# Sliding-window attention scores in a two-block network: masks written first, two score heads per row half, four PSUM banks in turn

## The chip, the cores and the metric

The program runs on one core of a Trainium2 chip. The metric is the device time of one execution in microseconds (us). TensorE (PE in the profile) multiplies, VectorE (DVE), ScalarE (ACT) and GpSimd (POOL) do the elementwise work, SyncE (SP) issues most transfers. PSUM, where TensorE writes, has eight banks of 512 fp32 columns on 128 partitions.

## The reference

Two blocks work on 512 tokens of width 1024. The first block (a linear-recurrence mixer, sparse attention and a mixture of 64 experts) is not touched. The second block has two layers, each of a feed-forward network, a hybrid mixer and another feed-forward network. The mixer projects the normalised tokens to eight query heads of 64, two key and two value heads of 64, a recurrence and a short convolution; the outputs are concatenated and multiplied with `w_out`. Its attention is:

```
scores = einsum('bnqkgd,bnskd->bnkgqs', qb, kb) * 64 ** -0.5      # blocks of 128 queries, 256 keys
scores = where(in_window & valid, scores - slope[head] * dist, -1e30)
m = max(max(scores), sink);  p = exp(scores - m);  denom = sum(p) + exp(sink - m)
out = (p / denom) @ vb
y = concatenate([y_attn, y_lru, y_shortconv]) @ w_out
```

A query sees the 128 keys up to itself, so a block of 128 queries needs its own block of keys and the one before it; the first block needs its own alone.

## The kernel before

The activations lie transposed (features on partitions, 512 tokens on columns). Products with weights are made of three fp32r products (`mm3`, L160, L161, L162): weights and activations are each split into a high and a low part, by a cast on ACT (L166) and a subtraction on DVE (L167). `fm` accumulates one 128x512 projection over eight slices in a bank: 24 products.

`mixer` (L1629) runs once a layer. It projects the recurrence inputs, keys and values, the queries and then, in a loop over four query blocks, calls `swa` (L1757). After it come the six projections of the short convolution (144 products into `ps_fm`), its elementwise work on DVE (L1740 to L1747), and `down` (L1560), the product with `w_out` into `ps_dn` banks; that takes the slices in the order 0 to 3 (attention), 6, 7 (short convolution), 4, 5 (recurrence), the first 256 tokens before the last 256.

The layout of `swa`: query head t of key group 0 lies on partitions 0 to 63 of tile t of `q` (`mxa` in the profile), head t + 4, of group 1, on partitions 64 to 127. `kk` holds the keys of group 0 and 1 on the same halves. So a score product uses 64 of the array's 128 rows, either the lower or the upper half. `swab` holds the masks with the distance penalty, in bf16; a product with the bf16 identity (`identb`) adds a mask to scores in PSUM.

For two heads at a time, `swa` takes one `ps_dn` bank. For each head it makes the score product (L1767, fp32, which the profile shows as two passes) and then the mask product (L1768). DVE takes the maximum (`swm`, L1769) and the bias (`swn`, L1770), ACT the exponential with its sum (L1773). When all eight heads are through, the probabilities are scaled (group 0 on DVE, L1787; group 1 in four pieces on ACT, L1785), transposed on PE into `ps_sm` (L1792), copied to `pt` (L1794, on DVE or ACT), and multiplied with the values into `ps_po` (L1798), where each product uses 64 of the array's columns. The result is split into the operands of `w_out`.

PSUM holds three `fm` banks, two `dn`, two `sm` and one `po` in this part of the program. A bank is taken in turn: a new tile of a tag waits until the oldest one's readers are done.

The order of instructions on each engine isn't that of the source: a scheduler sets it when the program is built. Engines then run their queues in that order. In the program before, the scheduler puts the scores between the projections of the short convolution: these are written after `swa` in the source, but run while the softmax of a bank is under way.

Of the kernel before, what the change touches and what calls it, by code (L numbers as in the profile page):

```python
# [14 lines left out]
AF = mybir.ActivationFunctionType  # L15
OP = mybir.AluOpType
AX = mybir.AxisListType
# [124 lines left out]
class Kern:  # L142
# [1609 lines left out]
    def swa(self, l, i, q, kk, v, swab):  # L1752

        nc, d = self.nc, self.dpool
        t_ = slice(i * 128, (i + 1) * 128)
        j0 = max(i - 1, 0)
        nj = i + 1 - j0  # L1757
        nk = nj * 128
        mx, nm, sm = (d.tile([128, 8], F32, name=n, tag=n, bufs=2) for n in ("swm", "swn", "sws"))
        pp = [self.m4.tile([128, 4, 256], F32, name="swp", tag="macc", bufs=3) for _ in range(2)]  # L1760
        for h in range(0, 8, 2):
            ps = self.bank("dn")[:, 0:2 * nk].rearrange("p (t k) -> p t k", t=2)
            g = h // 4
            gp = slice(g * 64, (g + 1) * 64)
            for a in range(2):
                t = (h + a) % 4
                nc.tensor.matmul(ps[:, a], q[gp, t, t_], kk[gp, j0 * 128:(i + 1) * 128], start=True, stop=False)  # L1767
                nc.tensor.matmul(ps[:, a], self.identb, swab[:, t, g, 256 - nk:256], start=False, stop=True)  # L1768
            nc.vector.tensor_reduce(mx[:, h:h + 2], ps, AX.X, OP.max)  # L1769
            nc.vector.scalar_tensor_tensor(nm[:, h:h + 2], mx[:, h:h + 2], -0.125, self.nsink[:, l, h:h + 2],  # L1770
                                           op0=OP.mult, op1=OP.min)
            for a in range(2):
                nc.scalar.activation(pp[g][:, (h + a) % 4, 0:nk], ps[:, a], AF.Exp, bias=nm[:, h + a:h + a + 1],  # L1773
                                     scale=0.125, accum_out=sm[:, h + a:h + a + 1])
        nc.vector.tensor_tensor(mx, nm, self.sink[:, l], OP.add)
        nc.scalar.activation(mx, mx, AF.Exp)
        nc.vector.tensor_tensor(sm, sm, mx, OP.add)
        nc.vector.reciprocal(sm, sm)
        pso = self.bank("po")
        for g in range(2):  # L1780
            gp = slice(g * 64, (g + 1) * 64)
            pv = pp[g][:, :, 0:nk]
            if g:
                for t in range(4):
                    nc.scalar.mul(pv[:, t], pv[:, t], sm[:, 4 + t:5 + t])  # L1785
            else:
                nc.vector.tensor_tensor(pv, pv, sm[:, 0:4, None].to_broadcast([128, 4, nk]), OP.mult)  # L1787
            pts = []
            for j in range(nj):
                pst = self.bank("sm")  # L1790
                for n, t in enumerate((0, 2, 1, 3)):
                    nc.tensor.transpose(pst[:, n * 128:(n + 1) * 128], pp[g][:, t, j * 128:(j + 1) * 128], self.ident)  # L1792
                pt = self.t2("pt")
                (nc.scalar.copy if j else nc.vector.tensor_copy)(pt, pst)  # L1794
                pts.append(pt)
            for b in range(2):
                for j in range(nj):
                    nc.tensor.matmul(pso[b * 64:(b + 1) * 64, g * 256:(g + 1) * 256], v[:, j0 + j, gp],  # L1798
                                     pts[j][:, b * 256:(b + 1) * 256], start=j == 0, stop=j == nj - 1)
        self.split(pso[:].rearrange("p (k s) -> p k s", k=4), self.ah[:, 0:4, t_], self.al[:, 0:4, t_])  # L1800
# [112 lines left out]
```

## Time and profile before

| | us |
|---|---|
| three runs | 3186.16, 3207.44, 3209.56 (median 3207.44) |
| the profiled execution | 3204.98 |
| its span, first to last instruction | 3203.2 |
| PE busy in the span | 3079.4 (96%) |
| DVE busy | 1874.3 (59%) |
| ACT busy | 1263.3 (39%) |

The profile is of one execution; times within it count from the start of the span. Busy is the time in which at least one instruction of an engine ran. PE starts a product before the one ahead of it has ended, so the time that one takes from the others is read from start to start, not from its duration. The chain that ended last is PE for 85% of the span. Score products of the two layers start from 1735.0 to 1802.7 us and again from 2697 us.

### The profile page before, as it was taken

Reading aid. Unit: us, or ns where it says so; the run is one execution under the profiler, and the core shown is the slowest. Engines: PE = TensorE matmul, PEld = TensorE weight load, DVE = VectorE, ACT = ScalarE, POOL = GpSimd, SP = SyncE. Lnnn points to the kernel's source line nnn. Section 1 sums busy time; section 2 is a strip of 40 time slices with the busy share of each in tenths; the row PEclk is TensorE's granted clock in tenths of the full one; section 3 lists DMA queues with packets and bytes.
Section 4 is the critical chain, followed back from the end, with each engine's and each line's share of the span. In section 5 each row is a group of like instructions: output and inputs, shape, how many; then the busy total and the mean of one; then the engine's idle time right before and its main releaser. Section 6 shows DMA issues by size and latency. Waiting matters only on the chain.

```text
span 3203.2 us, 40592 instructions
## 1 busy us (share of the span) xinstructions
PE 3079.4 (96%) x15628; PEld 2352.7 (73%) x15629; DVE 1874.3 (59%) x3048; ACT 1263.3 (39%) x2048; POOL 338.8 (11%) x373
## 2 busy tenths in 40 slices
PE   6999998999999996999999999999999989999999
PEld 5987477555555653888887788889888887788888
DVE  6776558777777765544485654345444485653335
ACT  5135554444445544322245542224322244542323
POOL 0111001322232322000010000000000010000000
PEclk9998799999999998999999999999999999999999
DMA  6574146999899996454372335344344372232323
GB/s 240 180 230 149 47 138 246 320 345 339 292 334 346 335 328 217 148 158 133 125 243 81 123 123 157 125 145 132 119 151 139 125 230 79 87 109 95 105 81 104
DMA packets 317574, 576.57 MB, mean 180 GB/s; under 512 B 49488, under 2 KB 252048, under 8 KB 292800
## 3 DMA queue, kind: packets, MB, share of 16 engines
q1 hardware_dynamic: 268656, 434.99, 39.3%
q0 software_dynamic: 46640, 136.84, 14.7%
q8 instruction: 125, 2.05, 0.3%
q10 hardware_dynamic: 2080, 2.10, 0.2%
q14 instruction: 73, 0.60, 0.1%
HBM read 550.84 MB, written 28.39 MB: 181 GB/s over the span
## 4 chain that ended last, share of the span: by engine, by line
PE 85%; DVE 5%; DMA 5%; issue 3%; ACT 1%; POOL 0%; SPq 0%; DVEq 0%; ACTq 0%; POOLq 0%
PE ps_fm L161 12%; PE ps_fm L162 12%; PE ps_fm L160 12%; PE ps_dn L1327 6%; PE ps_dn L160 6%; PE ps_dn L162 6%; PE ps_dn L161 6%; PE ps_gu L160 3%; PE ps_gu L161 3%; PE ps_gu L162 3%; PE ps_sc L876 2%; PE ps_tr L1297 2%; PE ps_pj L161 2%; PE ps_pj L160 2%; PE ps_pj L162 2%
## 5 line engine op out<-in xcount | busy, mean ns | idle before, releaser
L167 DVE TENSOR_TENSOR wlo<-wraw,whi 128x1024 fp32r<-128x1024 f32 x480 | 566.4, 1183 | 656.3 <-ACT whi L166 649.7
L166 ACT CAST whi<-wraw 128x1024 fp32r<-128x1024 f32 x480 | 487.0, 1017 | 860.8 <-PE ps_fm L161 366.9
L160 PE MATMUL ps_fm<-dhh,whi 128*128 128x512 f32 (+1 forms) x1808 | 675.9, 377 | 8.7 <-ACT dhh L1513 6.4
L161 PE MATMUL ps_fm<-dhl,whi 128*128 128x512 f32 (+1 forms) x1808 | 676.5, 375 | 3.0 <-DVE dhl L1514 2.5
L162 PE MATMUL ps_fm<-dhh,wlo 128*128 128x512 f32 (+1 forms) x1808 | 663.1, 375 | 1.1 <-DVE wlo L167 1.0
L160 PEld LDWEIGHTS ps_fm<-dhh,whi 128*128 128x128 f32 x1808 | 342.2, 190 | 70.2 <-ACT dhh L1513 7.3
L161 PEld LDWEIGHTS ps_fm<-dhl,whi 128*128 128x128 f32 x1808 | 343.4, 190 | 64.3 <-DVE dhl L1514 4.6
L160 PE MATMUL ps_dn<-ah,whi 128*128 128x256 f32 (+1 forms) x1152 | 383.8, 334 | 5.4 <-DVE xT L1590 5.4
L162 PEld LDWEIGHTS ps_fm<-dhh,wlo 128*128 128x128 f32 x1808 | 343.5, 190 | 61.2 <-DVE wlo L167 1.9
L161 PE MATMUL ps_dn<-al,whi 128*128 128x256 f32 (+1 forms) x1152 | 382.4, 332 | 0.0
L162 PE MATMUL ps_dn<-ah,wlo 128*128 128x256 f32 (+1 forms) x1152 | 380.3, 334 | 0.0
L167 DVE TENSOR_TENSOR wlo<-wbig,whi 128x1024 fp32r<-128x1024 f32 x192 | 232.1, 1220 | 94.8 <-ACT whi L166 94.4
L160 PEld LDWEIGHTS ps_dn<-ah,whi 128*128 128x128 f32 x1152 | 216.4, 188 | 30.6 <-DVE xT L1590 3.7
L166 ACT CAST whi<-wbig 128x1024 fp32r<-128x1024 f32 x192 | 198.9, 1047 | 95.8 <-PE ps_gu L162 77.7
L161 PEld LDWEIGHTS ps_dn<-al,whi 128*128 128x128 f32 x1152 | 216.6, 188 | 26.1 <-issue 1.5
L162 PEld LDWEIGHTS ps_dn<-ah,wlo 128*128 128x128 f32 x1152 | 216.3, 188 | 23.5 <-issue 0.8
L161 PE MATMUL ps_gu<-wlo,th 128*128 128x512 f32 (+21 forms) x512 | 210.2, 411 | 10.9 <-DVE wlo L167 10.9
L160 PE MATMUL ps_gu<-whi,th 128*128 128x512 f32 (+21 forms) x512 | 210.5, 412 | 2.0 <-ACT whi L166 1.8
L162 PE MATMUL ps_gu<-whi,tl 128*128 128x512 f32 (+21 forms) x512 | 202.8, 396 | 0.0
L1590 DVE SCALAR_TENSOR_TENSOR xT<-ps_dn,modc,xT 128x256 f32<-128x256 f32 (+1 forms) x160 | 93.7, 589 | 161.7 <-PE ps_dn L162 161.5
L1327 PE MATMUL ps_dn<-dnraw,eaf 128*80 128x512 f32 (+20 forms) x368 | 167.4, 596 | 0.5 <-ACT eaf L976 0.5
L1198 POOL DMA_INDIRECT ring<-h2d,iidx x64 | 96.0, 1500 | 381.6 <-PE ps_tr L1297 130.3
(533 smaller groups left out, 4112.2 us busy)
## 6 DMA issues: line engine op xcount, KB each, us to landing
wbig<-in_w_exp_gu_dram SPq DMA_DIRECT2D x96, 1024.0 KB, 14.5
wraw<-in_w_ffn_gu_dram SPq DMA_DIRECT2D x86, 1024.0 KB, 5.1
dnraw<-in_w_exp_dn_dram SPq DMA_DIRECT2D x48, 1024.0 KB, 10.1
mw<-in_w_mod_dram POOLq DMA_DIRECT2D x80, 512.0 KB, 4.4
mraw<-in_w_mod_dram POOLq DMA_DIRECT2D x64, 512.0 KB, 4.7
wraw<-in_w_exp_gu_dram SPq DMA_DIRECT2D x32, 1024.0 KB, 12.6
wraw<-in_w_ffn_down_dram SPq DMA_DIRECT2D x32, 1024.0 KB, 5.0
wraw<-in_w_out_dram SPq DMA_DIRECT2D x24, 1024.0 KB, 5.0
```

The source lines that it names most:

```text
L160: mm(ps, ah, bh, start=first, stop=False)
L161: mm(ps, ah, bl, start=False, stop=False)
L162: return mm(ps, al, bh, start=False, stop=last)
L166: self.copied = self.nc.scalar.copy(hi, src)
L167: self.rest = self.nc.vector.tensor_tensor(lo, src, hi.bitcast(F32), OP.subtract)
L876: nc.tensor.matmul(ps[:, 0:nk], qr[gp, t, t_], self.kr[b][gp, 0:nk], start=True, stop=False)
L1198: self.nc.gpsimd.indirect_dma_start(out=g[0:cap], out_offset=None, in_=self.h2d[:], in_offset=bass.IndirectOffsetOnAxis(ap=i_ap[0:cap], ax ...
L1297: nc.tensor.transpose(ps[:, k * 128:k * 128 + m], g[0:m, 4 * a + k:D:8], self.ident[0:m, 0:m])
L1327: self.mark2 = nc.tensor.matmul(ps[0:m], af[:, k, 0:m], dv[:, k, cs], start=k == 0, stop=k == 1)
L1590: self.hold = nc.vector.scalar_tensor_tensor(self.xT[:, k, hs], ps[j], G[:, k:k + 1], self.xT[:, k, hs], op0=OP.mult, op1=OP.add)
```

## The change

`swa` goes over the heads in two rounds (c = 0 and 1) of four: heads 2c and 2c + 1 of group 0 and the same of group 1 (t and t + 4). It takes two banks a round, one for each group: `ps_dn` in the first round, `ps_fm` in the second. One mask product (L1765) now writes the masks of a bank's two heads at once and opens the accumulation, 512 columns wide (256 in the first query block). Then the score products (L1769) are written a head of group 0 and a head of group 1 in turn. Maxima, biases and exponentials are the same instructions, in another order.

```diff
-        for h in range(0, 8, 2):
-            ps = self.bank("dn")[:, 0:2 * nk].rearrange("p (t k) -> p t k", t=2)
-            g = h // 4
-            gp = slice(g * 64, (g + 1) * 64)
+        for c in range(2):
+
+            pss = [self.bank("fm" if c else "dn")[:, 0:2 * nk].rearrange("p (t k) -> p t k", t=2) for _ in range(2)]
+            for g in range(2):
+                nc.tensor.matmul(pss[g], self.identb, swab[:, 2 * c:2 * c + 2, g, 256 - nk:256], start=True, stop=False)
             for a in range(2):
-                t = (h + a) % 4
-                nc.tensor.matmul(ps[:, a], q[gp, t, t_], kk[gp, j0 * 128:(i + 1) * 128], start=True, stop=False)
-                nc.tensor.matmul(ps[:, a], self.identb, swab[:, t, g, 256 - nk:256], start=False, stop=True)
-            nc.vector.tensor_reduce(mx[:, h:h + 2], ps, AX.X, OP.max)
...
+                for g in range(2):
+                    gp = slice(g * 64, (g + 1) * 64)
+                    nc.tensor.matmul(pss[g][:, a], q[gp, 2 * c + a, t_], kk[gp, j0 * 128:(i + 1) * 128], start=False,
+                                     stop=a == 1)
+            for g in range(2):
+                ps, h = pss[g], 4 * g + 2 * c
+                nc.vector.tensor_reduce(mx[:, h:h + 2], ps, AX.X, OP.max)
...
```

The scheduler makes a new order of it. PE, the start of the second query block of the first layer, before (`ps_dn_15193` is the block's first bank, 15490 and 15531 are projections of the short convolution):

```order
L1767 MATMUL ps_dn_15193<-kk_14635,mxa_14634 128x256
L1768 LDWEIGHTS identb_80
L1768 MATMUL ps_dn_15193<-swab_14636,identb_80 128x256
L1767 MATMUL ps_dn_15193<-kk_14635,mxa_14634 128x256
L1768 LDWEIGHTS identb_80
L1768 MATMUL ps_dn_15193<-swab_14636,identb_80 128x256
L161 MATMUL ps_fm_15490<-dhl_14563,whi_15461 128x512
L162 MATMUL ps_fm_15490<-dhh_14562,wlo_15462 128x512
L160 MATMUL ps_fm_15531<-dhh_14562,whi_15523 128x512
```

The same place in the changed program (`ps_dn_15189` and 15190 are the first round's banks for group 0 and 1, `ps_fm_15205` and 15206 the second round's):

```order
L1765 LDWEIGHTS identb_80
L1765 MATMUL ps_fm_15205<-swab_14636,identb_80 128x512
L1769 MATMUL ps_fm_15205<-kk_14635,mxa_14634 128x256 x2
L1765 LDWEIGHTS identb_80
L1765 MATMUL ps_dn_15189<-swab_14636,identb_80 128x512
L1769 MATMUL ps_dn_15189<-kk_14635,mxa_14634 128x256 x2
L1765 LDWEIGHTS identb_80
L1765 MATMUL ps_dn_15190<-swab_14636,identb_80 128x512
L1769 MATMUL ps_dn_15190<-kk_14635,mxa_14634 128x256 x2
L1765 LDWEIGHTS identb_80
L1765 MATMUL ps_fm_15206<-swab_14636,identb_80 128x512
L1769 MATMUL ps_fm_15206<-kk_14635,mxa_14634 128x256 x2
```

In the second, third and fourth query block each bank's two scores, both of one group, follow its mask, and the next bank's mask follows them; heads of the two groups do not stand next to each other. In the first query block they do (group 0, 1, 0, 1, with 128 columns). All sixteen banks' scores of a layer now stand together, with parts of the first two blocks' transposes and value products between them, and the first projection of the short convolution (`ps_fm_15449`) comes behind the last score:

```order
L1765 LDWEIGHTS identb_80
L1765 MATMUL ps_dn_15360<-swab_14636,identb_80 128x512
L1769 MATMUL ps_dn_15360<-kk_14635,mxa_14634 128x256 x2
L1802 MATMUL ps_po_15225<-pt_15254,mxa_14634 64x256
L160 MATMUL ps_fm_15449<-dhh_14562,whi_15441 128x512
L161 MATMUL ps_fm_15449<-dhl_14563,whi_15441 128x512
L162 MATMUL ps_fm_15449<-dhh_14562,wlo_15442 128x512
```

So the 144 projection products, which stood between the scores of all four blocks, have moved behind them. The first round's two masks of the first query block moved the other way: they run ahead of the projections of keys and queries, next to the products with `ones` (L205).

ACT, from the first exponential of the layer, in the changed program (in the program before, the conversion of weights for the projections and the copies of their results stood between these):

```order
L1777 ACT_TABLE_LOAD
L1777 ACTIVATE swp_15120,sws_15119<-ps_dn_15122,swn_15118 128x128 x2
L1777 ACTIVATE swp_15121,sws_15119<-ps_dn_15123,swn_15118 128x128 x2
L1777 ACTIVATE swp_15120,sws_15119<-ps_fm_15138,swn_15118 128x128 x2
L1777 ACTIVATE swp_15121,sws_15119<-ps_fm_15139,swn_15118 128x128 x2
L1777 ACTIVATE swp_15187,sws_15186<-ps_fm_15205,swn_15185 128x256
L1780 ACTIVATE swm_15117<-swm_15117 128x8
L1777 ACTIVATE swp_15187,sws_15186<-ps_fm_15205,swn_15185 128x256
L1777 ACTIVATE swp_15187,sws_15186<-ps_dn_15189,swn_15185 128x256 x2
```

The bank of `ps_dn_15122` has to be read before `ps_dn_15189` can be written: there are two `dn` banks.

## Rows read from the trace of the kernel before

**Rows 1.** Windows, both layers' scores: us, busy us (instructions) by engine, clock, DMA

```profile
1735.00:1803.00 68.00, 67.32 (x314) 44.21 (x313) 36.33 (x69) 33.19 (x94) 0.20 (x2) 1.00 0.19 63
2697.00:2765.00 68.00, 67.32 (x318) 44.44 (x318) 36.90 (x71) 31.86 (x93) 0.00 (x0) 1.00 0.17 58
```

**Rows 2.** Timeline, PE, first layer: start us, busy us, engine, line, operation, count

```profile
1748.62 0.39 PE L162 MATMUL ps_fm<-dhh,wlo 128*128 128x512 f32 x1
1748.85 0.39 PE L160 MATMUL ps_fm<-dhh,whi 128*128 128x512 f32 x1
1749.17 0.48 PE L1767 MATMUL ps_dn<-kk,mxa 64*128 64x128 f32 x2
1749.59 0.23 PE L1768 MATMUL ps_dn<-swab,identb 128*128 128x128 bf16 x1
1749.75 0.48 PE L1767 MATMUL ps_dn<-kk,mxa 64*128 64x128 f32 x2
...
1750.33 0.70 PE L1767 MATMUL ps_dn<-kk,mxa 64*128 64x256 f32 x2
1750.95 0.28 PE L1768 MATMUL ps_dn<-swab,identb 128*128 128x256 bf16 x1
1751.17 0.70 PE L1767 MATMUL ps_dn<-kk,mxa 64*128 64x256 f32 x2
...
1751.83 0.48 PE L161 MATMUL ps_fm<-dhl,whi 128*128 128x512 f32 x1
1752.15 0.39 PE L162 MATMUL ps_fm<-dhh,wlo 128*128 128x512 f32 x1
```

**Rows 3.** Timeline, PE, value products

```profile
1764.58 0.65 PE L1798 MATMUL ps_po<-pt,mxa 128*64 128x256 f32 x4
...
1801.24 0.65 PE L1798 MATMUL ps_po<-pt,mxa 128*64 128x256 f32 x2
```

**Rows 4.** Timeline, ACT, the first bank's exponentials (idle before, and what ended it)

```profile
1737.99 1.28 ACT L1773 ACT_TABLE_LOAD   x1 [1.51 <-DVE swn L1770]
1739.29 0.37 ACT L1773 ACTIVATE swp<-ps_dn,swn 128x128 f32<-128x128 f32 x1
...
1739.90 0.20 ACT L1773 ACTIVATION_READ_ACCUMULATOR swp<-ps_dn,swn 128x1 f32 x1
```

**Rows 5.** Timeline, DVE, the first bank's maximum; the short convolution's last product

```profile
1736.29 0.42 DVE L1769 TENSOR_REDUCE swm<-ps_dn 128x2 f32<-128x256 f32 x1 [1.79 <-PE ps_dn L1768]
1736.63 1.22 DVE L167 TENSOR_TENSOR wlo<-wraw,whi 128x1024 fp32r<-128x1024 f32 x1
1737.76 0.15 DVE L1770 SCALAR_TENSOR_TENSOR swn<-swm,nsink 128x2 f32<-128x2 f32 x1
...
1782.37 0.69 DVE L1747 TENSOR_TENSOR sc<-sc,ps_fm 128x512 f32<-128x512 f32 x1 [1.35 <-PE ps_fm L162]
1783.74 0.69 DVE L167 TENSOR_TENSOR al<-sc,ah 128x512 fp32r<-128x512 f32 x1 [0.69 <-ACT ah L166]
```

**Rows 6.** Groups, 1735 to 1830 us: count, busy us, mean ns, idle before

```profile
L1773 ACT ACTIVATE swp<-ps_dn,swn 128x256 f32<-128x256 f32 x24 | 11.2, 471 | 17.7 <-DVE swn L1770 15.8 <-DVE sws L1777 1.9
L1785 ACT ACTIVATE swp<-swp,sws 128x256 f32<-128x256 f32 x12 | 5.1, 504 | 0.0
...
L1769 DVE TENSOR_REDUCE swm<-ps_dn 128x2 f32<-128x512 f32 x12 | 8.3, 689 | 11.5 <-PE ps_dn L1768 11.5
L1794 DVE COPY pt<-ps_sm 128x512 f32<-128x512 f32 x8 | 5.5, 689 | 2.2 <-PE ps_dn L1768 1.3 <-PE ps_sm L1792 0.8
L1787 DVE TENSOR_TENSOR swp<-swp,sws 128x1024 f32<-128x1024 f32 x3 | 3.7, 1223 | 0.1
```

**Rows 7.** Timeline, first layer, ahead of the key projections

```profile
1675.41 3.52 POOL L1639 CAST swab<-sb 128x512 bf16<-128x512 f32 x4 [4.94 <-DVE macc L195]
...
1683.32 1.92 PE L205 MATMUL ps_po<-ones,macc 128*128 128x1 f32 x16 [0.59 <-DVE macc L195]
```

More of the change, by code (lines that the diff above doesn't have):

```diff
@@ L1760, in swa @@
         pp = [self.m4.tile([128, 4, 256], F32, name="swp", tag="macc", bufs=3) for _ in range(2)]
-        for h in range(0, 8, 2):
-            ps = self.bank("dn")[:, 0:2 * nk].rearrange("p (t k) -> p t k", t=2)
-            g = h // 4
-            gp = slice(g * 64, (g + 1) * 64)
+        for c in range(2):
+            pss = [self.bank("fm" if c else "dn")[:, 0:2 * nk].rearrange("p (t k) -> p t k", t=2) for _ in range(2)]
+            for g in range(2):
+                nc.tensor.matmul(pss[g], self.identb, swab[:, 2 * c:2 * c + 2, g, 256 - nk:256], start=True, stop=False)
             for a in range(2):
-                t = (h + a) % 4
-                nc.tensor.matmul(ps[:, a], q[gp, t, t_], kk[gp, j0 * 128:(i + 1) * 128], start=True, stop=False)
-                nc.tensor.matmul(ps[:, a], self.identb, swab[:, t, g, 256 - nk:256], start=False, stop=True)
-            nc.vector.tensor_reduce(mx[:, h:h + 2], ps, AX.X, OP.max)
[L1770 to L1774, printed above, removed]
+                for g in range(2):
[5 more added lines that the diff above has]
+                nc.vector.tensor_reduce(mx[:, h:h + 2], ps, AX.X, OP.max)
+                nc.vector.scalar_tensor_tensor(nm[:, h:h + 2], mx[:, h:h + 2], -0.125, self.nsink[:, l, h:h + 2],
+                                               op0=OP.mult, op1=OP.min)
+                for a in range(2):
+                    nc.scalar.activation(pp[g][:, 2 * c + a, 0:nk], ps[:, a], AF.Exp, bias=nm[:, h + a:h + a + 1],
+                                         scale=0.125, accum_out=sm[:, h + a:h + a + 1])
         nc.vector.tensor_tensor(mx, nm, self.sink[:, l], OP.add)
```

## Prediction, made before the change was run

> **What bounds the kernel now.** I read the page first: PE is busy for 96% of the span and carries 85% of the chain of waits, so a time can only come out of PE's queue. Then the windows around the scores of the two layers [rows 1]: in 68 us PE is busy for 67.3, at full clock, while DVE is busy for 44, ACT for 36 and DMA for a fifth. The reader is to see that there is hardly any idle time of PE to remove here; a gain must come from PE work that gets shorter, and a loss from PE time that gets idle. Then the timeline of PE inside that window [rows 2], read from start to start. The two layers differ little, so I work out one and double it.
>
> What the start-to-start times say [rows 2]: a score and its mask of 256 columns take .62 + .22 = .84 us (1750.33 to 1751.17), of 128 columns .42 + .16 = .58 (1749.17 to 1749.75). A projection product takes .23 (1748.62 to 1748.85); the last one ahead of a score takes .32 (1748.85 to 1749.17), .09 more. From 1751.17 to 1751.83 a score alone, with its mask behind, fits the .84 again. A score thus grows by .20 for 128 more columns, from .22 at none; a mask grows by .06, so one of 512 columns takes about .33 (an estimate: .22 + 2 x .055).
>
> **The change part by part, for one layer.**
>
> *Masks of twice the width, in the three blocks with 256 keys.* Before, a bank took 2 x .84 = 1.68. Now it takes one mask of .33 and two scores, of the same half of the array one behind the other, .22 + 2 x .41 = 1.04: 1.37 together. It saves .31 on each of 12 banks, **3.7 us**. If the change of form costs the scores their start-up twice, they take 1.24 and 1.3 us is saved; if the mask costs nothing extra over .22, 5.0. I take 3.7, since it holds to the increments of the rows.
>
> *The first block.* Before, 8 x .58 = 4.64. Now the first round's two masks run far ahead, where PE waited .59 us for DVE [rows 7] after POOL had cast the masks (1675.41 + 3.52, done 4 us earlier); that wait covers the .44. If the masks came later than that wait, they would cost .44. The second round's masks cost 2 x .22. The four scores of a round alternate between the halves of the array. No score of before does that. The nearest rows are the value products, which use 64 columns of the array instead of 64 rows: the stretches of four passes and of two are both busy for .65 [rows 3], so two halves ran side by side. If row halves do the same, a round of four takes .63 (.22 + 2 x .205) and the block 1.70: **2.9 us** saved. If they don't, 1.04 and 2.52: 2.1 saved.
>
> *Fewer entries.* Before, ten stretches of projections and five of `w_out` stood between the scores, transposes and value products, now five stretches stand between them. Each costs about .09 at entry [rows 2] and, I take it, as much at exit: 10 x .18 = 1.8. Part of them border on transposes, which use the whole array: **1.5 us**, with .9 to 1.8 for the ends.
>
> *The projections move behind the scores.* Their 144 products and their weights' conversion (casts on ACT, subtractions on DVE, transfers issued by SP) are the same in number; so are the maxima, exponentials and copies. The sum of PE work saved is 3.7 + 2.9 + 1.5 = **8.1 us a layer**. What goes is the cover: before, a softmax ran beside projections; now scores must cover it.
>
> *The first bank.* `dn` has two banks; the third bank of that tag, for the second block, waits until the first is read. From the first score: .63 and about .1 for the result; two maxima of .34 (1736.29 to 1736.63, [rows 5]); a subtraction of a weight's low part in between, 1.13; the bias to the start of the table load, .23; the load 1.30 and two exponentials with their sum .81 (1737.99 to 1739.29, and to 1740.10) [rows 4]. Together 4.9 us. PE has .63 + .44 + .63 + 1.37 = 3.07 before it needs the bank. Stall: **1.8 us**. The queue behind it is PE's own, and scores, transposes and value products all stand in it; DVE and ACT then have less to do, not more. If the subtraction runs elsewhere, the stall is .7.
>
> *Later stalls.* Value products now stand close behind the transposes that feed them, and wait for a copy out of PSUM, .69 [rows 6]. I count two such waits uncovered, **1.4 us**. Zero is the lower end; the upper end is the first rival.
>
> *`w_out` behind the last projection.* The short convolution's last product and its low part end 2.06 us after PE's last projection product (1782.37 to 1784.43, [rows 5]). The attention slices come first: 24 products at half of a projection's .23, some 2.8 us, run beside it. **Nothing**, and if another subtraction of 1.13 is queued ahead on DVE, .4.
>
> *The weights' transfers.* They start no earlier than before, and DMA is busy for a fifth [rows 1]; while the scores run the queue can fill, so I count nothing. If the raw buffers were all taken when the burst ends, the first projection would find its weights converted all the same: three conversions wait on nothing else.
>
> Net: 8.1 - 1.8 - 1.4 = 4.9 us a layer, **9.8 in all**. The profiled execution is 3204.98, so it would be 3195.2; the median of the runs is 2.5 higher, so 3197.6.
>
> **The rivals.**
>
> *Slower: the burst becomes bound by softmax, through five banks.* Within the burst a score bank (two `dn`, three `fm`) comes round every five banks, 5 x 1.37 = 6.9 us of PE. What DVE and ACT must do for a bank [rows 6]: a maximum .69, bias .2, two exponentials .94, together with sums some 2.1. In such a turn there are also a scaling of 1.22, two copies of .69 and four pieces of scaling of .50: 2.1 + 1.2 + 1.4 + 2.0 = 6.7. That is .2 less than the 6.9, if they stand one behind the other. Three more copies of .69 in the chain make it 8.8: PE then waits 1.9 in each turn, and sixteen banks are 3.2 turns: 6.1. With 1.8 and 1.4 from above it is 9.3 against 8.1: 1.2 slower a layer, 3207.4 for the profiled execution and **3210** for the median. It decides from the point at which PE's stalls exceed 8.1 us a layer. For it: the projections, behind which a bank's softmax ran, are out of the burst. Against it: before, DVE waited 11.5 us for scores ahead of the maxima alone [rows 6], and much of its 44 busy us is weight conversion, which mostly stands still in the burst; DVE and ACT share the chain. The Trainium skill (TensorEngine Tiling (Array Packing), PSUM Bottleneck and Gotcha 1) says the same in general: row tiling speeds up the products and not the emptying of PSUM, and more banks are wanted at once. No run here shows it yet. Chance .17.
>
> *No change: the stalls eat the gain.* Half of that, 3 us more of stalls a layer, and the forecast's first block without side-by-side halves (.8): about 1 us a layer left, **3205**. Chance .20.
>
> *More: halves side by side in all blocks.* If a bank of group 0 and the one of group 1 run at the same time, 2 x .82 become .82 for six pairs: 4.9 more a layer, **3188**. Against it stands the order: in three blocks a mask of full height lies between the groups. The Trainium skill (TensorEngine Tiling (Array Packing), Key Properties) says that tiles operate independently, but that a change of mode drains the engine; by that the mask keeps the groups apart, and the .09 at the entry of a score agrees with a small price of such a change. Chance .06.
>
> *It doesn't do what it says.* In three blocks the four banks aren't written in turn, as the words would have it; the forecast has that. If it fails in the first block also, the forecast loses .8 a layer, 1.6 in all: 3199, inside its range.
>
> **How the numbers follow.** The forecast has .57: 3197.6, its own range 3190 to 3205 by the bounds above (1.3 instead of 3.7, stalls .7 to 4). One of the three runs before was 21 us shorter without a row that shows why; since the result's runs may fall so too, I put the time at **3196** and let the range reach to 3178. Upwards it goes to 3213, the slower rival with its bounds. One per cent is 32 us, about what a measurement of this kernel can tell from no change: below 3175 or above 3239. All cases lie within it, so .91 for that, .05 for faster (more, with a run like the short one) and .04 for slower (stalls of over 16 us a layer beyond the saving).
>
> **What would show it.** In the profile after: 1.37 from the start of a wide mask to the next bank's mask; alternating scores of the first block at .63 for four; an idle time of PE near 1.8 before the first `dn` mask of the second block, ended by ACT's exponential; the stretch of 68 us [rows 1], from the first score to the start of `w_out`, 4.9 shorter, some 63 us, in both layers. It is wrong if PE shows more than 8 us of idle time there, if the wide bank takes 1.68 as before, or if the time goes in or out at `w_out`'s start or at the transfers.

## The result, and the profile after

The changed kernel takes 3218.3 us (median of 15 runs, 3195.68 to 3233.57) against 3201.61 us before (15 runs): the ratio over all runs is 1.0063, 95% interval 1.0044 to 1.0082. It is slower by about 20 us by that ratio (the medians alone differ by 16.7), where 10 us less had been forecast. Its profiled execution took 3208.22 us, with a span of 3205.7 us.

For each layer I take one stretch, from the first score to the first projection of the next feed-forward network. It holds the scores, the softmax, the projections of the short convolution and `w_out`, and begins and ends with the same work in every version. It is a better measure than the time of one execution: what lies ahead of the first score varies from run to run (the stretch of layer 1 starts at 1735.02 before, at 1723.19 in the changed kernel and at 1740.18 in a second profile of it). From the first score to the end of the span it is 1468.2 us before and 1482.5 after. Windows of that stretch in the kernel before, layer 1 and 2 (columns as in [rows 1]; the third from the right is the granted clock):

```profile
1735.02:1852.78 117.76, 117.08 (x716) 91.15 (x715) 70.95 (x129) 62.16 (x145) 3.34 (x8) 1.00 0.35 117
2695.29:2813.04 117.75, 117.07 (x715) 91.14 (x715) 70.95 (x129) 62.16 (x145) 0.00 (x0) 1.00 0.27 90
```

The same in the changed kernel:

```profile
1723.19:1852.46 129.27, 126.99 (x697) 97.96 (x697) 70.86 (x129) 61.97 (x145) 3.38 (x8) 0.85 0.32 106
2694.80:2815.20 120.40, 118.12 (x697) 93.60 (x697) 70.76 (x129) 61.72 (x145) 0.00 (x0) 0.93 0.27 88
```

The stretches got longer by 11.5 and 2.7 us, 14.2 together, which is all of the 14.3 from the first score on. PE waits little: its idle time is 2.3 us in each (129.27 - 126.99), against .7 before. What differs is the clock, whose mean fell from 1.00 to .85 and .93. Finer windows of the changed kernel, layer 1 and then layer 2:

```profile
1724.00:1726.00 2.00, 1.95 (x14) 1.20 (x13) 2.00 (x6) 0.67 (x3) 0.00 (x0) 1.00 1.03 331
1726.00:1728.00 2.00, 0.57 (x3) 0.26 (x2) 1.57 (x7) 1.99 (x6) 0.00 (x0) 0.94 0.50 166
1728.00:1730.00 2.00, 1.87 (x4) 1.16 (x4) 0.00 (x0) 2.00 (x13) 0.00 (x0) 0.50 0.00 0
...
1764.00:1766.00 2.00, 2.00 (x7) 0.95 (x5) 0.00 (x0) 1.60 (x5) 0.53 (x1) 0.67 0.00 0
1766.00:1768.00 2.00, 2.00 (x9) 1.35 (x9) 1.02 (x3) 2.00 (x8) 0.53 (x1) 1.00 0.72 186
...
2700.00:2702.00 2.00, 2.00 (x6) 0.92 (x5) 0.33 (x1) 2.00 (x13) 0.00 (x0) 0.64 0.00 0
...
2716.00:2718.00 2.00, 2.00 (x8) 0.64 (x7) 1.48 (x6) 2.00 (x9) 0.00 (x0) 0.59 0.00 0
```

By the means of these windows the clock of layer 1 goes from 1.00 (2.4 GHz) to .50 (1.2 GHz) at 1727.8, 4.6 us after the first score and within a wait of PE, and is back at 1765.3, among the last scores and ahead of the first projection. In layer 2 it falls at 2700.6, 5.8 us after the first score, and is back at 2717.6. But for its first five banks, nearly all of the burst of layer 1 runs at half speed. The timeline of PE there, changed kernel, and from 2717.76 on layer 2:

```profile
1723.19 0.71 PE L1769 MATMUL ps_dn<-kk,mxa 64*128 64x128 f32 x8
1723.84 0.39 PE L1765 MATMUL ps_fm<-swab,identb 128*128 128x256 bf16 x2
1724.16 1.03 PE L1769 MATMUL ps_fm<-kk,mxa 64*128 64x128 f32 x8
1725.12 0.39 PE L1765 MATMUL ps_fm<-swab,identb 128*128 128x512 bf16 x1
1725.44 1.13 PE L1769 MATMUL ps_fm<-kk,mxa 64*128 64x256 f32 x4
1728.13 0.59 PE L1765 MATMUL ps_dn<-swab,identb 128*128 128x512 bf16 x1 [1.56 <-ACT swp L1777]
...
1731.19 2.07 PE L1769 MATMUL ps_dn<-kk,mxa 64*128 64x256 f32 x4
1733.19 0.61 PE L1765 MATMUL ps_fm<-swab,identb 128*128 128x512 bf16 x1
...
2717.76 1.13 PE L1769 MATMUL ps_dn<-kk,mxa 64*128 64x256 f32 x4
2718.82 0.65 PE L1802 MATMUL ps_po<-pt,mxa 128*64 128x256 f32 x4
2719.40 0.39 PE L1765 MATMUL ps_fm<-swab,identb 128*128 128x512 bf16 x1
2719.72 0.48 PE L1769 MATMUL ps_fm<-kk,mxa 64*128 64x256 f32 x1
```

Two scores of 256 columns take 2.00 us at half clock (1731.19 to 1733.19) and 1.06 where the clock is back (2717.76 to 2718.82). The one wait of note, 1.56 us, is the one forecast at 1.8. What the low clock costs can be estimated from these times: half of 37.5 us (1727.8 to 1765.3) is 18.8, half of 17.0 (2700.6 to 2717.6) is 8.5, if PE works all the while; in layer 1 it waits for about 1 us of it. Without that the stretches would be 110.5 and 111.9, that is 7.3 and 5.9 shorter than before, where the forecast had 4.9. So the forecast gain is there by this estimate, and a loss of 27 us on the clock covers it.

### The profile page after: what moved, and what is told of

The parts are those of the page before. It is cut to its first block, busy times and chain, and to the rows that moved or that the text cites. A ratio compares the mean times of both kernels' runs of the same rounds, so it can differ in the third digit from the quotient of the medians.

```text
span 3205.7 us, 40502 instructions
## 1 busy us (share of the span) xinstructions
PE 3080.1 (96%) x15596; PEld 2356.4 (74%) x15597; DVE 1874.5 (58%) x3048; ACT 1263.0 (39%) x2048; POOL 338.3 (11%) x373
## 4 chain that ended last, share of the span: by engine, by line
PE 86%; DVE 6%; DMA 4%; issue 3%; ACT 1%; POOL 0%; SPq 0%; DVEq 0%; POOLq 0%; ACTq 0%
PE ps_fm L161 12%; PE ps_fm L162 12%; PE ps_fm L160 12%; PE ps_dn L1327 6%; PE ps_dn L160 6%; PE ps_dn L162 6%; PE ps_dn L161 6%; PE ps_gu L160 3%; PE ps_gu L161 3%; PE ps_gu L162 3%; PE ps_pj L161 2%; PE ps_pj L160 2%; PE ps_pj L162 2%; PE ps_tr L1297 2%; PE ps_sc L876 2%
```

## The experiments

The theory after this reading: before, projections stood between the scores; the scores now stand together, and in such a burst the clock falls. The main rivals: the wide masks or the alternating halves lower it by themselves; waits for banks eat the gain (the slower rival of the prediction); the wait of PE in which layer 1's clock fell lowers it. All ratios are to the kernel before, with 95% intervals; a run without one was timed once.

**Projections back, by banks.** Both rounds take `dn` banks, so the scores must wait for them, and the scheduler puts projections between.

```diff
-            pss = [self.bank("fm" if c else "dn")[:, 0:2 * nk]...
+            pss = [self.bank("dn")[:, 0:2 * nk]...
```

> The change with one tag altered: both rounds take dn banks, none takes fm. The scores then wait for two banks, and the projections stand between them again (11 stretches). Theory (a burst of scores without projections lets TensorE's clock fall): granted clock 1.00 from the first score to w_out in both layers, first score to the next feed-forward's first projection 117.8 - 5 to 7 = 111 to 113 us (before 117.8, changed 129.3 and 120.4), whole time .995 to .998 of before. Rival one (masks of 512 columns or alternating row halves lower the clock by themselves): the clock falls here as in the changed kernel, 120 or more in that stretch, 1.005. Rival two (waits for banks eat the gain, the clock apart): clock 1.00 but 117 or more.

Windows of the two stretches:

```profile
1728.39:1840.18 111.79, 110.53 (x697) 89.52 (x697) 69.84 (x129) 61.69 (x145) 3.37 (x8) 1.00 0.37 123
2682.49:2794.48 111.99, 110.53 (x698) 89.58 (x697) 69.71 (x129) 61.69 (x145) 0.00 (x0) 1.00 0.29 95
```

The clock stays at 1.00, with the same masks and halves. 111.8 and 112.0 us are what the theory had; the whole time, .9982 (.9964 to 1.0000), 3192.78 us, is at the edge of what it had.

**Projections back, by the source's order.** The banks stay as in the change.

```diff
-        for i in range(4):
-            self.swa(l, i, q, kk, v, swab)
+        self.swa(l, 0, q, kk, v, swab)
         ... proj2(1536) ...
+        self.swa(l, 1, q, kk, v, swab)
         ... proj2(1792) ...
+        self.swa(l, 2, q, kk, v, swab)
         ... proj2(1280), its elementwise work ...
+        self.swa(l, 3, q, kk, v, swab)
```

> The change with its banks as they are (dn and fm in turn), but the source calls the four query blocks between the three pairs of projections of the short convolution instead of ahead of all. Theory (the clock falls since projections are missing between the scores): clock 1.00 in the stretch, 110 to 113 us from the first score to the next feed-forward's first projection in both layers, .994 to .997 of before. Rival one (masks or row halves lower the clock): it falls, 120 or more, 1.005. Rival two (waits): clock 1.00, 117 or more.

Window of layer 1 (layer 2 has the same 107.07):

```profile
1724.70:1831.77 107.07, 107.02 (x698) 87.36 (x698) 70.26 (x129) 61.52 (x145) 3.35 (x8) 1.00 0.40 128
```

Clock 1.00, and PE waits for .05 us in 107. The stretch is 10.7 shorter than before, below the 110 to 113 expected. The whole time is 3171.02 us, **.9909 (.9878 to .9940)**, also better than expected: this beats both kernels. Its timeline shows part of why, in the last query block:

```profile
1776.25 0.60 PE L1766 MATMUL ps_dn<-swab,identb 128*128 128x512 bf16 x2
1776.79 1.14 PE L1770 MATMUL ps_dn<-kk,mxa 64*128 64x256 f32 x8
1777.85 0.61 PE L1766 MATMUL ps_fm<-swab,identb 128*128 128x512 bf16 x2
```

Here both masks come first, and four scores (eight passes) take 1.06 us, as long as two of one half: the halves run side by side.

**More pairs.** Each score is also held behind its round's second mask.

```diff
+                msk = nc.tensor.matmul(pss[g], self.identb, ...   # the last of the two masks
...
+                    with self.after(msk):
                         nc.tensor.matmul(pss[g][:, a], q[gp, 2 * c + a, t_], ...
```

> The version with projections between, and each score product held behind the mask of its round's second bank, so that the heads of both groups may stand next to each other in more blocks. Theory (row halves run side by side wherever no product of full height lies between, .43 for a pair of 256 columns): stretch from the first score to the next feed-forward's first projection 105 to 106.5 us against 107.07, clock 1.00, whole time .988 to .993 of before. Rival (the scores now wait for the second bank, and the wait takes back what the halves give): 107 to 109 us.

```profile
1716.82:1822.46 105.64, 105.59 (x698) 86.50 (x697) 70.09 (x129) 61.43 (x145) 3.35 (x8) 1.00 0.39 130
```

The stretch (window of layer 1) is 1.43 shorter again. The whole time, 3171.92 us or .9905 (.9870 to .9939), can't be told from that of the version above.

**The burst without the change.** The kernel before takes `fm` for two of its four pairs; masks, heads and halves are as before.

```diff
-            ps = self.bank("dn")[:, 0:2 * nk]...
+            ps = self.bank("fm" if h in (2, 6) else "dn")[:, 0:2 * nk]...
```

> The kernel before, narrow masks and head by head, with fm banks for the second and fourth pair of heads: the scores of a layer stand together as in the changed kernel, nothing else of the change is in it. Theory (the burst lowers the clock): clock at .50 for 15 to 45 us in each layer, 122 to 135 us from the first score to the next feed-forward's first projection, 1.004 to 1.012 of before. Rival one (wide masks or alternating halves do it): clock 1.00, 114 to 118 us, .998 to 1.002.

Windows, the fall in layer 1 and then the stretch of each layer:

```profile
1720.00:1721.00 1.00, 1.00 (x6) 0.68 (x5) 0.47 (x2) 0.87 (x1) 0.00 (x0) 1.00 0.99 335
1721.00:1722.00 1.00, 1.00 (x6) 0.56 (x5) 0.42 (x1) 0.99 (x4) 0.00 (x0) 0.70 0.04 10
1722.00:1724.00 2.00, 2.00 (x5) 1.09 (x5) 0.80 (x5) 1.55 (x10) 0.00 (x0) 0.50 0.00 0
...
1717.16:1844.92 127.76, 127.45 (x715) 96.19 (x715) 71.53 (x129) 61.89 (x145) 3.35 (x8) 0.91 0.33 108
2686.28:2814.04 127.76, 127.45 (x715) 96.24 (x715) 71.56 (x129) 61.90 (x145) 0.00 (x0) 0.91 0.25 83
```

The clock falls with nothing of the change but the burst: 127.76 us in both layers, whole time 1.0090 (1.0052 to 1.0127). In layer 1 it is at .50 for 24 us, from 1721.4, 4.2 us after the first score. The reader is to see that PE was busy in all of each slice when the clock fell; no wait came ahead of it. The Trainium skill (TensorE: Matmul & The Clock Gate, Part 1) says that the clock gate follows how busy the engine has been; by the profile's busy share this row differs, and the measurement decides: a busy PE in the page isn't a sign that the clock holds.

**The wide masks alone,** in the kernel before.

```diff
+            nc.tensor.matmul(ps, self.identb, swab[:, h % 4:h % 4 + 2, g, 256 - nk:256], start=True, stop=False)
             for a in range(2):
-                nc.tensor.matmul(ps[:, a], q[gp, t, t_], ..., start=True, stop=False)
-                nc.tensor.matmul(ps[:, a], self.identb, swab[:, t, g, 256 - nk:256], start=False, stop=True)
+                nc.tensor.matmul(ps[:, a], q[gp, t, t_], ..., start=False, stop=a == 1)
```

> The kernel before with one mask product a bank, written first, and nothing else: dn banks, head by head, no alternating halves. My sum's first term alone: .31 on each of 16 banks, 4.9 us a layer, so 112.4 to 113.4 us from the first score to the next feed-forward's first projection against 117.76, clock 1.00, .996 to .999 of before. Rival (masks were hidden beside the scores, or two scores of a half take 1.24): 115.5 to 118 us.

```profile
1727.37:1840.59 113.22, 112.98 (x698) 90.95 (x698) 70.39 (x129) 62.10 (x145) 3.35 (x8) 1.00 0.37 121
```

4.5 us less a layer (window of layer 1), on average .28 on each of 16 banks, where .31 was expected. Whole time .9982 (.9959 to 1.0005).

**What in the burst does it?** The scores use 64 of the array's 128 rows. In the next runs their number of rows is changed; the attention then computes other values, so these runs answer for the time alone.

```diff
-                    nc.tensor.matmul(pss[g][:, a], q[gp, 2 * c + a, t_], kk[gp, j0 * 128:...
+                    nc.tensor.matmul(pss[g][:, a], q[:, 2 * c + a, t_], kk[:, j0 * 128:...
```

> The changed kernel, but each score product reads all 128 partitions of keys and queries, so it adds the other group's scores (the attention's values differ). Same order, same number of columns and passes; only the first block loses the side-by-side halves, .8 us a layer. Theory in its narrower form (it is the half-filled array that makes the burst look idle): clock 1.00 through the burst, 112 to 114 us from the first score to the next feed-forward's first projection, .996 to .999. Rival in that place (the wait of 1.5 us at the first dn bank, or fp32 products whatever their rows): the clock falls as in the changed kernel, 120 to 130 us, 1.004 to 1.008.

Window of layer 1, and PE in the burst:

```profile
1737.40:1847.46 110.06, 107.21 (x697) 91.96 (x696) 70.25 (x129) 61.58 (x145) 3.38 (x8) 1.00 0.37 125
```

```profile
1742.45 0.38 PE L1765 MATMUL ps_dn<-swab,identb 128*128 128x512 bf16 x1 [1.67 <-ACT swp L1777]
1742.67 1.02 PE L1769 MATMUL ps_dn<-kk,mxa 128*128 128x256 f32 x4
1743.53 0.38 PE L1765 MATMUL ps_dn<-swab,identb 128*128 128x512 bf16 x1
```

The clock stays at 1.00 in the same burst, behind the same wait (1.67 us), with as many columns and passes: 110.06 us, whole time .9951 (.9930 to .9972). So the wait isn't what lowers it; in the kernel before with `fm` banks the clock fell with no wait ahead. But the stretch is also shorter than the 112 to 114 expected: a bank takes 1.08 here (1742.45 to 1743.53) instead of 1.38, now that mask and scores have one form (both on the whole array). Fewer changes of form, between whole and half array, might be why the clock holds.

The burst of the kernel before, on all rows (the same edit there):

> The kernel before with fm banks for the second and fourth pair, and with scores that read all 128 partitions (the attention's values differ). Theory (half-filled rows in a burst lower the clock): clock 1.00 where the version on half the rows had .50 for 24 us in each layer, 109 to 116 us in the stretch against 127.76. Rival (any burst of fp32 scores lowers it): .50 again, 122 to 128 us.

```profile
1736.06:1846.38 110.32, 108.74 (x716) 91.98 (x715) 70.92 (x129) 61.47 (x145) 3.37 (x8) 1.00 0.37 125
```

Clock 1.00, 110.32 against 127.76 on half the rows.

**Rows or changes of form?** The next four runs ask this. First, the changed kernel without its mask products:

> The changed kernel with the mask products left out (the attention then sees all keys): the burst holds scores on 64 rows and no change between the whole array and its halves except at transposes and value products. Theory (half-filled rows let the clock fall): .50 again in each layer, within 2 to 6 us of the first score, 108 to 125 us in the stretch. Rival (what counts is the changes between whole and half array, with the gaps of .1 us that they leave): clock 1.00 until the scores end, 103 to 107 us.

```profile
1713.94:1821.68 107.74, 103.71 (x684) 88.86 (x684) 69.54 (x129) 61.45 (x145) 2.83 (x7) 0.98 0.37 123
```

Mean clock .98, 107.74 us: close to the rival, and just outside what the theory had. The scores of both groups, with no mask between, run partly side by side here, so the run doesn't separate the two. Second, all rows, and ahead of each score a product of 8 columns on half of them:

```diff
+                    nc.tensor.matmul(pss[g][:, a, 0:8], q[gp, 2 * c + a, t_], kk[gp, j0 * 128:j0 * 128 + 8], ...
                     nc.tensor.matmul(pss[g][:, a], q[:, 2 * c + a, t_], kk[:, j0 * 128:...
```

> The version with scores on all rows, and ahead of each score a product of 8 columns on 64 rows into the same bank (the attention's values differ), which brings 32 changes between whole and half array back per layer and more. Theory (half-filled rows over many columns): clock 1.00, 115 to 122 us in the stretch, the added products' own time. Rival (the changes between whole and half array): .50 in both layers, 130 us or more.

```profile
1727.66:1859.88 132.22, 132.22 (x761) 106.17 (x761) 71.68 (x129) 62.35 (x145) 3.36 (x8) 0.91 0.32 104
```

The clock fell (.93 and 129.25 us in layer 2): a miss for the theory, though the scores fill the array. The added products are no clean test either, since they are many and each fills little; which part of them lets the clock fall, no run shows. The last two take one thing at a time. No masks, and the scores of both groups on the lower half, so that nothing can run side by side and the form changes only at transposes and value products:

```diff
-                    gp = slice(g * 64, (g + 1) * 64)
+                    gp = slice(0, 64)
```

> As the run without masks, but the scores of both groups read partitions 0 to 63 (the attention's values differ, and no masks are added): nothing can run side by side, half of the array stays empty through the scores, and the array's form changes only at transposes and value products. Theory (half-filled rows lower the clock; the run without masks got off since its halves overlapped): .50 for 12 us or more in each layer, 112 us or more in the stretch. Rival (changes of form lower it): 5 us of .50 or less, 106 to 109 us.

```profile
1712.00:1716.00 4.00, 3.16 (x21) 2.52 (x20) 2.95 (x8) 2.45 (x3) 0.00 (x0) 1.00 0.79 260
1716.00:1754.00 38.00, 35.83 (x98) 24.36 (x99) 16.77 (x44) 19.47 (x76) 0.53 (x1) 0.51 0.05 15
...
1712.08:1837.14 125.06, 122.05 (x683) 100.74 (x683) 70.51 (x129) 61.94 (x145) 2.85 (x7) 0.85 0.32 106
```

.51 for 38 us, 125.06 in the stretch (layer 2: mean .87, 121.56). And scores on all rows with masks on the lower half, so that the form changes at every bank as in the changed kernel:

```diff
-                nc.tensor.matmul(pss[g], self.identb, swab[:, 2 * c:2 * c + 2, g, ...
+                nc.tensor.matmul(pss[g], self.identb[0:64], swab[0:64, 2 * c:2 * c + 2, g, ...
```

> As the version with scores on all rows, but each mask product uses the lower 64 rows (half of the masks is missing, and the attention's values differ): as many changes between whole and half array as in the changed kernel, no products added, and the scores fill the array. Theory (half-filled rows over the scores' columns): clock 1.00 or .50 for less than 5 us, 110 to 114 us. Rival (the changes of form): .50 for 12 us or more in each layer, 118 us or more.

```profile
1729.17:1842.23 113.06, 110.66 (x698) 91.10 (x697) 70.59 (x129) 61.74 (x145) 3.36 (x8) 1.00 0.37 121
```

```profile
1734.23 0.37 PE L1765 MATMUL ps_dn<-swab,identb 64*128 64x512 bf16 x1 [1.22 <-ACT swp L1777]
1734.53 1.13 PE L1769 MATMUL ps_dn<-kk,mxa 128*128 128x256 f32 x4
1735.60 0.39 PE L1765 MATMUL ps_dn<-swab,identb 64*128 64x512 bf16 x1
```

Clock 1.00 throughout (layer 2: 113.07 us), and the bank takes 1.37 us again (1734.23 to 1735.60), so products follow as slowly as in the changed kernel's banks at full clock. So the changes of form cost .3 us a bank but don't lower the clock here; scores on half the rows, one behind the other, do. They aren't the only mix that does: the run with the added products stays unexplained. The Trainium skill (TensorEngine Tiling (Array Packing), Key Properties) says that a change of mode drains the engine; 1.37 against 1.08 would be its price for a bank with one change each way, if the drain is what costs it; no run parts the two.

**Once more the changed kernel.**

> The changed kernel once more, for another profile. Theory (its clock falls in each layer a few us after the first score, and comes back at no fixed product): clock at .50 in both layers again, 15 to 40 us of it, 118 to 130 us in the stretch. Rival (the fall came by chance into that one profile): clock 1.00, 110 to 113 us.

```profile
1740.18:1869.24 129.06, 126.78 (x697) 97.83 (x697) 70.85 (x129) 61.94 (x145) 3.38 (x8) 0.85 0.32 106
2711.48:2831.89 120.41, 118.13 (x698) 93.69 (x698) 70.77 (x129) 61.83 (x145) 0.00 (x0) 0.93 0.27 88
```

The fall is no chance of one profile. That the clock would come back at no fixed place was wrong: the stretches of the two profiles agree within .21 and .01 us. Why layer 2 gets it back some 20 us sooner than layer 1, with the same order of products, stays open.

## Why the prediction was wrong

The time lies 5 us above the range, and the sign is wrong. The interval also shows that a change of .6 per cent can be told here, where the prediction took one per cent. By its steps:

- **Wide masks, 3.7 us.** Right: a bank takes .32 + 1.06 = 1.38 at full clock (2719.40 to 2719.72, 2717.76 to 2718.82), forecast 1.37. Alone, with the first block's, they give 4.5.
- **First block, 2.9 us.** Nearly: the first round's four scores take .65 (1723.19 to 1723.84), side by side as taken from the value products [rows 3]; the second round's take .96, since a gap stands between its pairs. From first to last 1.93 against 1.70.
- **Fewer entries, 1.5 us.** No run takes this term alone. Its half for the exits doesn't fit its own rows: score, mask and the first projection behind them take .98 (1751.17 to 1752.15, [rows 2]), not more than the .62 + .22 + .23 = 1.07 of the three by themselves but less.
- **First bank's stall, 1.8 us.** 1.56, ended by ACT's exponential as forecast; the low part's subtraction and the table load do stand in the chain. Of the later stalls, 1.4 in the sum, .7 showed.
- **`w_out`, nothing.** Right: no wait of PE there; the stretch's idle time is these two waits.
- **The slower rival, softmax through five banks.** Wrong: it wanted more than 8 us of waits a layer, and there are 2.3. The right sign was put on the wrong mechanism.
- **More, halves side by side in all blocks.** In the changed kernel the masks do keep them apart. With both masks first they run together, 1.06 for four scores, so the gain was real for another order.
- **The projections move behind the scores.** This is the step that failed. It asked what the move does to the cover of softmax and to the queues of DVE, ACT and SP, and priced all of it at stalls of PE. It took the durations of [rows 2], read at a clock of 1.00, as if they came along to the new place. In the place of that term the runs show about 18.8 us (layer 1) and 8.5 us (layer 2) of lost clock. The number to look at stood in [rows 1]: 1.00 belonged to that mix of products, with projections on the whole array among the scores.

The net at full clock was, by the estimate above, under-, not overestimated: about 6 to 7 us a layer against 4.9. With projections back between the scores, and PE's clock held, 10.7 a layer came out.

## What to carry to other kernels

A start-to-start time holds at the clock of the row that it is read from; when a change takes full-array products away from between products that use half the rows, price the whole stretch at the lower clock as a rival of its own. Before moving products for the sake of waits, ask what stands between them that keeps the array full, and let the scheduler have it there: here the order of four calls in the source brought the stretch from 129 and 120 us to 107. Products on the two row halves overlapped here only where nothing of full height stood between. Writing both masks first, as the change does, isn't enough, since the scheduler put a bank's scores right behind its own mask: hold the scores behind the second mask (1.43 us a layer in the stretch, though the whole time doesn't show it).

## What the runs showed of the hardware that was not expected

- PE busy in every slice, and yet its clock fell to .50, 4.2 us after the first score (1717.16 to 1721.4, kernel before with `fm` banks); the same burst on 128 rows kept 1.00.
- In the same order of products the clock came back 37.5 us after the fall in layer 1 and 17 us in layer 2, with nearly the same stretches in two profiles of the changed kernel (129.27 and 129.06; 120.40 and 120.41).
- A change between whole and half array costs .3 us a bank, either way round (1.38 with masks whole and scores half, 1.37 the other way, 1.08 with both whole).
